# The first stage of a hybrid encoder layer on one core: VectorE's order, the order of the loads, and twenty identity products

## The chip, the cores and the metric

The kernel runs on one core of a Trainium2 chip. The metric is the device time of one execution in microseconds (us). The median of three runs before the change is 2615.54 us, from 2612.58 to 2616.66.

## The reference, cut to what matters

One layer: a layer norm whose scale and shift come from a conditioning vector, one wide input projection, two mixing branches, an output projection, and a second norm.

```python
c_act = jax.nn.silu(c)
mod = c_act @ ada_w[l] + ada_b[l]                      # (1, 3072)
shift, scale, gate = jnp.split(mod, 3, axis=-1)
h = (_layernorm(x) * (1.0 + scale[:, None, :]) + shift[:, None, :]).astype(x.dtype)
proj = h @ w_in[l]                                     # (2048, 9216)
...
y_hg = _hgrn2_branch(q_h, i_h, zf_fw, zf_bw, g_h, ...)  # gated linear recurrence, 8 heads
o_na = _neighbourhood_attention(q_n, k_n, v_n, rpb[l])  # 16 heads, done in 8 pairs
y = jnp.concatenate([y_hg, y_na], axis=-1) @ w_out[l]
x = (_layernorm(DEEPNORM_ALPHA * x + gate[:, None, :] * y) * ln_g[l] + ln_b[l])
```

There are 2048 tokens of width 1024. Every projection is done in three passes for precision: an operand is split into a high part `hi` (its rounded copy) and a low part `lo` (the rest), and the products hi·hi, hi·lo and lo·hi are summed.

## The kernel before, in words

The span of 2610.9 us falls into a first stage (`startup`, until about 98 us), the neighbourhood attention of the first token half, the recurrence, the attention of the second half, and the output projection. The change touches `startup` alone.

`startup` makes the normed, modulated input `h` of the first 1024 tokens, and uses it as it comes. The tokens are in two groups of 512, g = 0 and 1, each of four rows of 128 tokens; the width is cut into eight blocks k = 0 to 7 of 128. For a group there are four x tiles for each half a of the width (a = 0 serves k = 0 to 3, a = 1 serves k = 4 to 7).

What is done for one (g, k):

- `turn_`: four PE transposes of the x tiles into PSUM (L232).
- `high`: ScalarE applies the modulation's `scale1[k]` and `shift[k]` (L237), and copies the result to the high part of h (L239).
- `low`: VectorE subtracts, which gives the low part of h (L1223).
- `block(g, k)`: nine products of 128x512 for the k, q and gate columns of the first pair of attention heads, by L278, into accumulators `acc`.
- one piece of `vproj`, the value projection, twelve products of 128x256 (L291).

PE runs in the order of the program. In iteration (g, k) the program first runs `jobs[g, k]`, then `ahead()`, that is `turn_`, `high` and `low` of the *next* (g, k), and then the block and the value piece of this one. So the next h is made on ScalarE and VectorE while PE works on this one. At (0, 7) come also fourteen products for the next pair's weights (`fourth_mm`, L1281), and the second group's rates and scaling.

What the jobs hold:

- `mod_sum(k)`: VectorE's row sums of a 128x2048 tile of modulation weights, in two instructions (L154), which give `shift[k]` and `scale1[k]`. `high(g, k)` waits for it.
- `w_split(i, a)`: ScalarE's copy (L1199) and VectorE's subtraction (L1200) for half a of the weights of column group i (three groups, six splits).
- `feed.split`: the same for a tile of the value weights (L825, L826); it also issues the load of a later tile.
- `stat`, `rates`, `scale`: the norm. `stat(g, i)` is VectorE's statistics of row i (L202, L203), `rates` the small work on mean and variance, `scale` normalizes x tiles in place, on ScalarE (L225) for rows below its third argument and on VectorE (L227) for the others.

Inside this stage PE, SP, ScalarE and VectorE are held to the program's order:

```python
with phase("st", SB_, SMS), tc.manual_schedule(engines={getattr(mybir.EngineType, e) for e in ("PE", "SP", "Activation", "DVE")}):
    raws, feed, first = startup()
with phase("n0", NB0, SM0):
    natten_init(4, 0)
    st = first_half(raws, feed, first)
```

All loads go through SP's queue. In the stages behind it only PE is held to the program; for the other engines a planner orders the instructions by a timeline of its own (`schedule_with_timeline_sim=True`), and it may place such instructions between those of the first stage.

The modulation tiles `ada` have four buffers. The first holds a diagonal used early, `mod_load(0)` to `(2)` take the others, `mod_load(3)` the first again, and `mod_load(4)` to `(7)` each wait for the `mod_sum` four places earlier.

Of the kernel before, what the change touches and what calls it, by code (L numbers as in the profile page):

```python
# [19 lines left out]
P = 128  # L20
# [18 lines left out]
def body(ctx: ExitStack, tc: tile.TileContext, t):  # L39
    nc = tc.nc  # L40
    dve, act, pool, pe = nc.vector, nc.scalar, nc.gpsimd, nc.tensor
# [46 lines left out]
    def nm(s):  # L88
        cnt[0] += 1
        return f"{s}_{cnt[0]}"  # L90

    def tl(tag, dt=F32, shape=None):
        if tag in cur["smap"]:
            tag = cur["smap"][tag]
            return sh.tile([P, 512], dt, tag=tag, name=nm(tag), bufs=SH[tag])
        return cur["pool"].tile([P, 512] if shape is None else shape, dt, tag=tag, name=nm(tag), bufs=cur["bufs"].get(tag, 1))
# [4 lines left out]
    def ps(tag="mx"):  # L101
        if tag == "pj":
            return pp.tile([P, 512], F32, tag=tag, name=nm("pj"))
        tag = cur["map"].get(tag, tag)
        return cur["psum"].tile([P, 512], F32, tag=tag, name=nm("ps"), bufs=cur["ps"][tag])
# [4 lines left out]
    ident = cp.tile([P, P], F32, name="ident")  # L110
# [36 lines left out]
    def mod_load(k):  # L147
        mod["w", k] = tl("ada", shape=[P, 2 * D])
        dma(mod["w", k], t["ada_m"][k])

    def mod_sum(k):
        for s, (dst, bias) in enumerate(((shift, adab), (scale1, adab1))):
            w, c = mod["w", k][:, s * D:(s + 1) * D], slice(k, k + 1)
            dve.tensor_tensor_reduce(w, w, mod["c"], scale=1.0, scalar=bias[:, c], op0=ALU.mult, op1=ALU.add, accum_out=dst[:, c])  # L154
# [34 lines left out]
    def x_load(g, rows=range(4)):  # L189
        xs = []  # L190
        for i in rows:
            xt = [tl("x"), tl("x")]
            r0 = g * GRP + i * P
            for a in range(2):
                dma(xt[a], x[r0:r0 + P, a * 512:(a + 1) * 512])
            xs.append(xt)
        return xs
# [14 lines left out]
    def x_mv():  # L212
        return cp.tile([P, 4, 2], F32, tag="xmv", name=nm("xmv"), bufs=2)
# [972 lines left out]
    def startup():  # L1186

        dma(adab, t["ada_b"])
        ws = [([], []) for _ in NCOL0]
        wraw = [[tl("raw"), tl("raw")] for _ in NCOL0]  # L1190
        feed = Chunks(first_srcs())

        def w_load(a):
            for i in range(3):
                dma(wraw[i][a], t["w_in"][NCOL0[i][1] // P][:, a * 512:(a + 1) * 512])

        def w_split(i, a):
            hi, lo = tl(f"w{i}", F32R), tl("w2l" if i == 2 else f"w{i}", F32R)
            act.activation(hi, wraw[i][a], AF.Copy)  # L1199
            dve.tensor_tensor(lo, wraw[i][a], hi, op=ALU.subtract)  # L1200
            ws[i][0].append(hi)
            ws[i][1].append(lo)

        mod_silu()
        xs, mvs, how, pts, tmps = {0: x_load(0)}, {0: x_mv()}, {}, {}, {}
        mod_load(0)
        w_load(0)
        feed.load(1)
        mod_load(1)
        mod_load(2)  # L1210
        feed.load(2)
        mod_load(3)
        w_load(1)
        feed.load(3)

        def turn_(g, k):
            pts[g, k] = h_turn(xs[g], k)

        def high(g, k):
            tmps[g, k] = h_high(pts[g, k], k, hts[g, k, 0], True)  # L1220

        def low(g, k):
            dve.tensor_tensor(hts[g, k, 1], tmps[g, k], hts[g, k, 0], op=ALU.subtract)  # L1223

        def stat(g, i):
            x_stat(mvs[g], xs[g], i)

        def rates(g):
            how[g] = x_rates(mvs[g])

        def scale(g, a, n, rows=range(4)):
            x_scale(xs[g], how[g], a, n, rows)

        for i in range(4):
            stat(0, i)
        rates(0)
        scale(0, 0, 4)
        mod_sum(0)

        jobs = {  # L1240
            (0, 0): [(w_split, 1, 0), (w_split, 2, 0), (feed.split, 0), (mod_sum, 1), (mod_sum, 2)],
            (0, 1): [(feed.split, 0), (scale, 0, 1, 4, (0, 1)), (mod_sum, 3)],
            (0, 2): [(w_split, 0, 1), (scale, 0, 1, 4, (2, 3))],
            (0, 3): [(mod_sum, 4), (w_split, 1, 1), (w_split, 2, 1)],
            (0, 4): [(feed.split, 0), (mod_sum, 5)],
            (0, 5): [(mod_sum, 6), (stat, 1, 0), (feed.split, 0)],
            (0, 6): [(lambda: fourth_split(),), (mod_sum, 7), (stat, 1, 1)],
            (0, 7): [(stat, 1, 2), (stat, 1, 3), (rates, 1), (scale, 1, 0, 2)],
            (1, 2): [(scale, 1, 1, 4)],
        }  # L1250
        mod_load(4)
        xs[1], mvs[1] = x_load(1, (0, 1)), x_mv()
        feed.load(4)
        mod_load(5)
        xs[1] += x_load(1, (2, 3))
        mod_load(6)
        mod_load(7)
        acc = {(0, 0): ps("sc"), (1, 0): ps("sc"), (2, 0): ps("po")}
        values = vproj(t["w_v"][0], nv_d[0], 0, feed, True)
        rows = {n: [None, None] for n, _ in NCOL0}  # L1260
        order = [(g, k) for g in range(2) for k in range(KT)]
        fourth, fraw = ([], []), [tl("raw"), tl("raw")]
        for a in range(2):
            dma(fraw[a], t["w_in"][NCOL0[0][1] // P + 1][:, a * 512:(a + 1) * 512])

        def fourth_split():
            w = tl("ada", F32R, [P, 2 * D])
            for a in range(2):
                hi, lo = (w[:, o:o + 512] for o in (a * 512, D + a * 512))
                act.activation(hi, fraw[a], AF.Copy)  # L1270
                fourth[0].append(hi)
                fourth[1].append(lo)

        def fourth_low():
            for a in range(2):
                dve.tensor_tensor(fourth[1][a], fraw[a], fourth[0][a], op=ALU.subtract)

        def fourth_mm(pz, k, low):
            wh, wl = (w[k // 4][:, (k % 4) * P:(k % 4 + 1) * P] for w in fourth)
            for n, (a, b) in enumerate(((wl, hts[0, k, 0]),) if low else ((wh, hts[0, k, 0]), (wh, hts[0, k, 1]))):  # L1280
                pe.matmul(pz, a, b, start=(k + n + low == 0), stop=(low == 1 and k == KT - 1))  # L1281

        def block(g, k):
            for i in (2, 0, 1) if g else (0, 1, 2):
                proj_mm(acc[i, g], *ws[i], g, k)
                if k == KT - 1:
                    rows[NCOL0[i][0]][g] = evac(acc[i, g])

        turn_(0, 0)
        high(0, 0)  # L1290
        w_split(0, 0)
        low(0, 0)
        for n, (g, k) in enumerate(order):
            if (g, k) == (0, 7):
                pz = ps("po")
                for kx in range(KT - 1):
                    fourth_mm(pz, kx, 0)
                block(g, k)
            for f, *a in jobs.get((g, k), []):
                f(*a)  # L1300
            nxt = order[n + 1] if n + 1 < len(order) else None

            def ahead():
                if nxt:
                    turn_(*nxt)
                    high(*nxt)
                    low(*nxt)

            if (g, k) != (0, 7):
                ahead()  # L1310
            if (g, k) == (0, 7):
                feed.load(8)
                rp = bias_rows()
                bias_fill()
                dma(lg, t["lb_logits"])
                dma(normg, t["hg_norm_g"])
            if (g, k) == (1, 0):
                acc.update({(2, 1): ps("po"), (0, 1): ps("sc"), (1, 1): ps("sc")})
                bias_tables(rp)
                bias_pair(0)  # L1320
                dma(c_d.rearrange("(p k) -> p k", k=KT), mod["c8"])
            if (g, k) != (0, 7):
                block(g, k)
            if (g, k) == (0, 7):
                next(values)
                fourth_mm(pz, k, 0)
                fourth_low()
                ahead()
                for kx in range(KT):
                    fourth_mm(pz, kx, 1)  # L1330
                first = evac(pz)
                next(values)
            else:
                next(values, None)
            if g:
                feed.tick()
        for _ in values:
            pass
        return rows, feed, first
# [98 lines left out]
    with psum_phase("n0", NPS), tc.manual_schedule(engines={mybir.EngineType.PE}):  # L1438
        with phase("st", SB_, SMS), tc.manual_schedule(engines={getattr(mybir.EngineType, e) for e in ("PE", "SP", "Activation", "DVE")}):
            raws, feed, first = startup()  # L1440
# [151 lines left out]
    with psum_phase("n1", NPS), phase("n1", NB1, SM1), tc.manual_schedule(engines={mybir.EngineType.PE}):  # L1592
# [13 lines left out]
        feed = Feed(cts)  # L1606
# [95 lines left out]
```

## Time and profile before

| | us |
|---|---|
| median of three runs | 2615.54 |
| lowest, highest | 2612.58, 2616.66 |
| the profiled execution's own time | 2612.69 |
| its span, first to last instruction | 2610.9 |
| PE busy, share of the span | 2561.6, 98% |
| PE busy in the first 100 us | 80.62 |
| VectorE busy in the first 100 us | 62.48 |
| ScalarE busy in the first 100 us | 56.74 |
| modulation weights loaded in the first stage | 8 tiles of 1024 KB |

In rows of the timeline the columns are the start in us, the duration in us, the engine (PE TensorE's matmuls, PEld its weight loads, DVE VectorE, ACT ScalarE, SPq SP's queue), the line of the kernel, the operation, what it writes and reads, and, in brackets, how long the engine was idle just before and what ended that. A row with x3 merges three instructions that follow each other. A row of the chain of waits gives start, length and what the chain went through. A row of the stretches gives the length, and for each engine busy us and instructions, then the granted TensorE clock (PEclk), the DMA engines' share, and GB/s.

### The profile page before, as it was taken

What the parts mean: (1) busy time and instruction counts of PE and PEld (TensorE: products, weight loads), DVE (VectorE), ACT (ScalarE), POOL (GpSimd) and SP (SyncE); (2) the same over time, 40 slices, a digit from 0 to 9 for tenths busy, and PEclk for the clock granted to TensorE, in tenths of its full rate; (3) what the DMA queues carried; (4) which work ended last, traced back from release to release, by engine and by line L of the source; (5) the groups of instructions that cost most, each with busy time, mean ns of one, the idle gap of its engine ahead of it and who ended that gap; (6) DMA issues with size and microseconds to landing.
All of it is one profiled execution on the core that took longest, in us unless ns stands there. A gap on an engine that the chain in (4) does not pass through costs nothing.

```text
span 2610.9 us, 45808 instructions
## 1 busy us (share of the span) xinstructions
PE 2561.6 (98%) x17140; PEld 2146.3 (82%) x17140; DVE 1737.8 (67%) x4356; ACT 1435.4 (55%) x2859; POOL 108.4 (4%) x143
## 2 busy tenths in 40 slices
PE   7999999999999999999999999999999999999998
PEld 5788788878888888888888888898888887788887
DVE  7445545377777778877887777555777778558443
ACT  5533444376666666666766666455777777431110
POOL 0000000000000000000000000000000000042221
PEclk9999999999999999999999999999999999999999
DMA  7576454212111126212212222345455556443331
GB/s 282 149 205 150 129 175 152 95 46 74 62 65 61 62 73 219 81 53 78 65 63 68 74 77 74 112 126 153 127 139 135 147 143 171 125 151 129 97 97 56
DMA packets 225919, 296.40 MB, mean 114 GB/s; under 512 B 28839, under 2 KB 117543, under 8 KB 224551
## 3 DMA queue, kind: packets, MB, share of 16 engines
q1 hardware_dynamic: 225695, 293.46, 37.0%
q8 instruction: 135, 2.21, 0.4%
q14 instruction: 89, 0.73, 0.1%
HBM read 218.18 MB, written 66.99 MB: 109 GB/s over the span
## 4 chain that ended last, share of the span: by engine, by line
PE 90%; DVE 4%; DMA 3%; ACT 2%; issue 1%; SPq 0%; DVEq 0%; ACTq 0%
PE pj L278 51%; PE pj L291 5%; PE ps L1527 4%; PE ps L1528 4%; PE ps L1529 4%; PE ps L1112 3%; PE ps L1090 3%; PE ps L482 2%; PE ps L1041 2%; PE ps L474 2%; PE ps L549 1%; PE ps L573 1%; PE ps L1048 1%; PE ps L575 1%; PE ps L521 1%; PE ps L653 1%
## 5 line engine op out<-in xcount | busy, mean ns | idle before, releaser
L278 PE MATMUL pj<-h,wh 128*128 128x512 f32 x3984 | 1269.9, 400 | 3.6 <-ACT wh L825 1.9
L278 PEld LDWEIGHTS pj<-h,wh 128*128 128x128 f32 x3984 | 722.7, 188 | 155.5 <-issue 14.0
L278 PE MATMUL pj<-h,wl 128*128 128x512 f32 x1992 | 781.2, 392 | 0.0
L278 PEld LDWEIGHTS pj<-h,wl 128*128 128x128 f32 x1992 | 374.5, 188 | 83.3 <-DVE wl L826 0.4
L1062 ACT ACTIVATE pbuf<-pbuf,mx 128x480 f32<-128x480 f32 (+5 forms) x256 | 152.4, 597 | 107.6 <-DVE mx L1057 106.6
L291 PE MATMUL pj<-wh,h 128*128 128x256 f32 x1024 | 196.2, 286 | 0.6 <-ACT vt L299 0.3
L1057 DVE CUSTOM_DVE_ANT_1 pbuf<-ps,bias 128x480 f32<-128x480 f32 (+5 forms) x256 | 129.1, 540 | 99.3 <-PE ps L1046 43.8
L291 PEld LDWEIGHTS pj<-wh,h 128*128 128x128 f32 x1024 | 163.3, 192 | 4.4 <-issue 1.3
L269 DVE TENSOR_TENSOR wl<-wr,wh 128x512 fp32r<-128x512 f32 x192 | 131.2, 684 | 48.2 <-ACT wh L268 46.6
L268 ACT ACTIVATE wh<-wr 128x512 fp32r<-128x512 f32 x192 | 120.2, 626 | 74.4 <-PE pj L278 66.8
L291 PE MATMUL pj<-wl,h 128*128 128x256 f32 x512 | 144.9, 283 | 0.0
L1096 ACT ACTIVATE pt<-ps 120x384 f32<-120x384 f32 (+3 forms) x128 | 65.2, 509 | 121.0 <-PE ps L1090 120.7
L1090 PE MATMUL ps<-ident,pbuf 128*128 128x128 f32 (+2 forms) x832 | 113.5, 274 | 4.0 <-DVE pbuf L1067 3.1
L1094 DVE COPY pt<-ps 120x384 f32<-120x384 f32 (+3 forms) x128 | 74.9, 585 | 63.5 <-PE ps L1090 62.3
L1090 PEld LDWEIGHTS ps<-ident,pbuf 128*128 128x128 f32 (+2 forms) x832 | 97.2, 137 | 22.1 <-issue 2.5
L468 DVE TENSOR_TENSOR de<-e,de 128x512 f32<-128x512 f32 x64 | 44.2, 691 | 95.2 <-ACT de L467 95.2
L1503 ACT ACTIVATE yh<-yr 128x512 fp32r<-128x512 f32 x52 | 32.7, 628 | 131.9 <-PE ps L1528 114.7
L1067 DVE TENSOR_SCALAR pbuf<-pbuf,mx 128x480 f32<-128x480 f32 (+5 forms) x256 | 101.0, 412 | 3.8
L1576 DVE TENSOR_TENSOR vt<-ps,gt 128x512 f32<-128x512 f32 x24 | 16.5, 691 | 129.2 <-PE ps L1529 129.2
L774 ACT ACTIVATE e<-pj 128x512 f32<-128x512 f32 x97 | 57.8, 596 | 80.4 <-PE pj L278 73.7
L291 PEld LDWEIGHTS pj<-wl,h 128*128 128x128 f32 x512 | 98.2, 192 | 1.4 <-issue 0.5
L449 DVE TENSOR_TENSOR_SCAN c<-c,g 128x128 f32<-128x128 f32 x256 | 88.4, 404 | 10.7 <-ACT c L439 10.7
(281 smaller groups left out, 4694.1 us busy)
## 6 DMA issues: line engine op xcount, KB each, us to landing
wr<-in_w_in SPq DMA_DIRECT2D x276, 256.0 KB
yr<-yq SPq DMA_DIRECT2D x64, 256.0 KB
bias<-tint SPq DMA_DIRECT2D x24, 480.0 KB
x<-in_x SPq DMA_DIRECT2D x32, 256.0 KB
ada<-in_ada_m SPq DMA_DIRECT2D x8, 1024.0 KB
wr<-in_w_v SPq DMA_DIRECT2D x32, 256.0 KB
nv<-vt SPq DMA_DIRECT2D x32, 256.0 KB
hs<-s SPq DMA_DIRECT2D x32, 256.0 KB
```

Of the source, the lines that this page charges most:

```text
L268: act.activation(hi, raw, AF.Copy)
L269: dve.tensor_tensor(lo, raw, hi, op=ALU.subtract)
L278: pe.matmul(pz, a, b, start=(k == 0 and n == 0), stop=(k == KT - 1 and n == 2))
L291: pe.matmul(pzs[tp][:, i * 256:(i + 1) * 256], a, b, start=(k == 0 and n == 0 and i == 0), stop=(k == KT - 1 and n == 2), skip_group_check ...
L449: dve.tensor_tensor_scan(c[:, sl], c[:, sl], L[:, sl], 0.0, op0=ALU.add, op1=ALU.subtract)
L1057: return dve.tensor_tensor_reduce(s[:, 0:nk].rearrange("p (r c) -> p r c", c=kw), sc[:, 0:nk].rearrange("p (r c) -> p r c", c=kw), bt[:, 0 ...
L1062: act.activation(s[:, 0:nk], s[:, 0:nk], AF.Exp, scale=-1.0, bias=mx[:, 0:1], accum_out=mx[:, 1:2])
L1067: dve.tensor_scalar(s[:, 0:nk], s[:, 0:nk], mx[:, 2:3], 1.0, op0=ALU.mult, op1=ALU.mult)
L1090: pe.transpose(ptp[0:cw, c * P:(c + 1) * P], s[:, c * cw:(c + 1) * cw], ident)
L1527: pe.matmul(pz, yh[:, kk], wh, start=first, stop=False)
L1528: pe.matmul(pz, yh[:, kk], wl, start=False, stop=False)
L1529: pe.matmul(pz, yl[:, kk], wh, start=False, stop=last)
```

## The change

Four things, all in `startup`:

1. The first four x tiles (a = 0, group 0) are scaled by ScalarE (rows 0 and 1) and VectorE (rows 2 and 3), not all by ScalarE. The second group's a = 1 tiles are scaled by VectorE, two at (1, 1) and two at (1, 2), not four by ScalarE at (1, 2).
2. The jobs stand in another order. The splits of the first two weight groups and `mod_sum(1)` come ahead of the first `low`; `mod_sum(2)` to `(7)`, the other splits and the statistics move between iterations.
3. `mod_load(6)` and `(7)` are issued ahead of the second group's rows 2 and 3.
4. In iteration (0, 0), behind the transposes of k = 1 and ahead of block (0, 0), PE computes 20 products of the 128x128 identity with itself, in float32, into a part of `acc[0, 0]`, which the block's first product then overwrites.

```diff
-        scale(0, 0, 4)
+        scale(0, 0, 2)
         mod_sum(0)
 
         jobs = {
-            (0, 0): [(w_split, 1, 0), (w_split, 2, 0), (feed.split, 0), (mod_sum, 1), (mod_sum, 2)],
-            (0, 1): [(feed.split, 0), (scale, 0, 1, 4, (0, 1)), (mod_sum, 3)],
-            (0, 2): [(w_split, 0, 1), (scale, 0, 1, 4, (2, 3))],
-            (0, 3): [(mod_sum, 4), (w_split, 1, 1), (w_split, 2, 1)],
-            (0, 4): [(feed.split, 0), (mod_sum, 5)],
-            (0, 5): [(mod_sum, 6), (stat, 1, 0), (feed.split, 0)],
-            (0, 6): [(lambda: fourth_split(),), (mod_sum, 7), (stat, 1, 1)],
+            (0, 0): [(w_split, 2, 0), (feed.split, 0)],
+            (0, 1): [(mod_sum, 2), (feed.split, 0), (scale, 0, 1, 4), (mod_sum, 3)],
+            (0, 2): [(mod_sum, 4)],
+            (0, 3): [(w_split, 0, 1), (w_split, 1, 1), (w_split, 2, 1), (feed.split, 0)],
+            (0, 4): [(mod_sum, 5), (mod_sum, 6)],
+            (0, 5): [(mod_sum, 7)],
+            (0, 6): [(feed.split, 0), (lambda: fourth_split(),), (stat, 1, 0), (stat, 1, 1)],
             (0, 7): [(stat, 1, 2), (stat, 1, 3), (rates, 1), (scale, 1, 0, 2)],
-            (1, 2): [(scale, 1, 1, 4)],
+            (1, 1): [(scale, 1, 1, 0, (0, 1))],
+            (1, 2): [(scale, 1, 1, 0, (2, 3))],
         }
         mod_load(4)
         xs[1], mvs[1] = x_load(1, (0, 1)), x_mv()
         feed.load(4)
         mod_load(5)
-        xs[1] += x_load(1, (2, 3))
         mod_load(6)
         mod_load(7)
+        xs[1] += x_load(1, (2, 3))
...
+        w_split(0, 0)
+        w_split(1, 0)
         turn_(0, 0)
         high(0, 0)
-        w_split(0, 0)
+        mod_sum(1)
         low(0, 0)
...
             if (g, k) != (0, 7):
                 ahead()
+            if (g, k) == (0, 0):
+                for _ in range(20):
+                    pe.matmul(acc[0, 0][:, 0:P], ident, ident, start=True, stop=True, skip_group_check=True)
```

## The prediction

> **What bounds the kernel now.** I read the page first (busy shares), then the stretches of the first 60 us, then the timeline of PE, VectorE and ScalarE there, then the chain of waits.
>
> ```profile
> span 2610.9 us, 45808 instructions
> PE 2561.6 (98%) x17140; PEld 2146.3 (82%) x17140; DVE 1737.8 (67%) x4356; ACT 1435.4 (55%) x2859; POOL 108.4 (4%) x143
> 0.00:20.00 20.00, 6.95 (x13) 2.93 (x13) 11.19 (x27) 8.87 (x17) 1.33 (x10) 1.00 0.84 316
> 20.00:40.00 20.00, 18.51 (x101) 15.98 (x101) 18.31 (x31) 12.02 (x20) 0.00 (x0) 1.00 1.04 405
> ```
>
> PE is busy for 98% of the span, so the whole kernel is PE-bound, and only PE's idle or slow time can be won. 13.05 of the 49.3 us without PE work lie in the first 20 us. From 20 to 40 us VectorE is nearly full (18.31 of 20) and the DMA engines are full (1.04). Three limits stand close together there.
>
> ```profile
> 17.02 1.33 PE L232 MATMUL ps<-ident,x 128*128 128x128 f32 x5 [0.23 <-ACT x L225]
> 20.87 1.22 PE L278 MATMUL ps<-h,bk 128*128 128x512 f32 x2 [0.54 <-DVE h L1223]
> 24.45 0.41 PE L291 MATMUL pj<-wh,h 128*128 128x256 f32 x1
> 25.73 0.28 PE L291 MATMUL pj<-wl,h 128*128 128x256 f32 x1
> 28.11 0.73 PE L278 MATMUL ps<-h,bk 128*128 128x512 f32 x2 [0.95 <-DVE h L1223]
> 39.73 0.94 PE L278 MATMUL ps<-h,bk 128*128 128x512 f32 x3
> 43.68 1.35 PE L278 MATMUL ps<-h,bk 128*128 128x512 f32 x3
> 49.30 0.73 PE L278 MATMUL ps<-h,bk 128*128 128x512 f32 x2 [0.58 <-DVE h L1223]
> 55.88 0.84 PE L278 MATMUL ps<-h,bk 128*128 128x512 f32 x3
> ```
>
> These are starts of blocks. Block (0, 0) runs from 20.87, and a value product takes 0.41 us at 24.45 but 0.28 us at 25.73: TensorE worked at a slower rate until about 25.5 us, 4.6 us after its dense work began. Block (0, 1) could go on only at 28.11, when VectorE delivered its low part. Block (0, 5) at 43.68 needs 1.35 us for three products where (0, 4) needs 0.94, a wait of 0.41 us. At 49.30 block (0, 6) waits for VectorE too. In between PE never waits.
>
> ```profile
> 71.78 0.60 PE L232 MATMUL ps<-ident,x 128*128 128x128 f32 x4
> 74.29 0.28 PE L291 MATMUL pj<-wh,h 128*128 128x256 f32 x1
> 75.72 0.60 PE L232 MATMUL ps<-ident,x 128*128 128x128 f32 x4
> 79.52 0.28 PE L291 MATMUL pj<-wh,h 128*128 128x256 f32 x1
> 72.52 2.92 ACT L225 ACTIVATE x<-x,xb,xr 128x512 f32<-128x512 f32 x4
> ```
>
> An undisturbed iteration takes 75.72 - 71.78 = 3.94 us; from its transposes to the value piece are 74.29 - 71.78 = 2.51 us. The next one needs 79.52 - 75.72 = 3.80 us: 1.29 us are lost, since `high(1, 3)` stood behind four scalings on ScalarE (72.52 for 2.92 us).
>
> **The change, part by part.** *The start.* The rows of ScalarE and VectorE:
>
> ```profile
> 14.04 2.93 ACT L225 ACTIVATE x<-x,xb,xr 128x512 f32<-128x512 f32 x4 [1.02 <-DVE xb L209]
> 17.54 0.78 ACT L237 ACTIVATE sg<-ps,shift,scale 128x512 f32<-128x512 f32 x1 [0.57 <-PE ps L232]
> 18.34 0.63 ACT L239 ACTIVATE h<-sg 128x512 fp32r<-128x512 f32 x1
> 25.13 0.78 ACT L237 ACTIVATE sg<-ps,shift,scale 128x512 f32<-128x512 f32 x1 [4.08 <-DVE scale L154]
> 20.13 0.68 DVE L1223 TENSOR_TENSOR h<-sg,h 128x512 fp32r<-128x512 f32 x1
> 20.74 0.68 DVE L1200 TENSOR_TENSOR q<-e,q 128x512 fp32r<-128x512 f32 x1
> 26.16 1.28 DVE L154 CUSTOM_DVE_ANT_0 ada<-ada,nb,adab 128x1024 f32<-128x1024 f32 x1
> 27.37 0.68 DVE L1223 TENSOR_TENSOR h<-sg,h 128x512 fp32r<-128x512 f32 x1
> 59.96 1.00 DVE L227 TENSOR_SCALAR x<-x,xmv,xr 128x512 f32<-128x512 f32 x2
> ```
>
> From them: a scaling is 0.73 us on ScalarE and 0.50 on VectorE; a subtraction occupies VectorE for 0.61 us (20.13 to 20.74), half a `mod_sum` for 1.21 (26.16 to 27.37), a whole one 2.42; `high` takes 0.80 + 0.63 = 1.43.
>
> After the change VectorE scales two tiles from 14.0 to 15.0 and then does `mod_sum(0)` until 17.45. ScalarE scales the other two until 15.5, then copies two weight tiles until about 16.7 (0.6 us each, like L239's copy). So the transposes end earlier, but `high(0, 0)` now waits for `mod_sum(0)` and starts at 17.5, as before (17.54): nothing won by that edit itself. VectorE goes on: two weight subtractions until 18.7, `mod_sum(1)` until 21.1, `low(0, 0)` until 21.8, one us later than before (20.13 + 0.68 = 20.81). But `scale1[1]` is there at 21.1, not just before 25.13, so `high(0, 1)` ends at 22.6, VectorE's two subtractions come between, and `low(0, 1)` ends at 23.6, not at 28.05 (27.37 + 0.68). Block (0, 1)'s wait of 0.95 us goes.
>
> *The loads.* `mod_sum(1)` needs its tile by 18.7.
>
> ```profile
> x<-in_x SPq DMA_DIRECT2D x32, 256.0 KB
> ada<-in_ada_m SPq DMA_DIRECT2D x8, 1024.0 KB
> 26.68 7.79 DMA ada<-in_ada_m
> ```
>
> In the queue's order there stand eight x tiles, `ada` 0, four tiles of 256 KB, `ada` 1 and `ada` 2: 6.3 MB, and 20 us at 316 GB/s is 6.3 MB. So `ada` 2 lands near 20 us and `ada` 1, 1.05 MB earlier, near 17.4: in time, by 1.3 us. The chain has the load issued at 26.68, `ada` 5, landing at 34.47. With 6 and 7 now right behind it, at 405 GB/s (2.6 us each), they land near 37.1 and 39.7; their sums start near 40.2 and 43.3. The second group's rows 2 and 3, pushed back 5.2 us to about 42.3, are read only behind 49 us. SP's queue now holds `mod_load(7)` behind `mod_sum(3)` (near 29.1), and x rows, the fourth group's tiles and later value tiles stand behind it; a load issued at 26.68 lands only 7.79 us later, so the engines have work until SP goes on, and it costs nothing.
>
> *The identity products.* The trace has float32 products of 128x128x128 in the recurrence, two records each:
>
> ```profile
> 870.11 1.06 PE L482 MATMUL ps<-v,ke 128*128 128x128 f32 x8
> 871.00 0.60 PE L474 MATMUL ps<-ident,de 128*128 128x128 f32 x4
> ```
>
> Four products in 871.00 - 870.11 = 0.89 us: 0.223 us each at the full rate, 0.445 at half. Twenty cost 4.46 or 8.9 us. The transposes take (1.33 - 0.45) / 4 = 0.22 us at that hour, so eight from 15.0, two of them held by ScalarE, end near 17.15, and the products follow at once. If the rate rises 4.6 us after dense work begins, as at 25.5 before, 10.3 products run slowly, 9.7 fast, and the last ends at 17.15 + 4.6 + 2.16 = 23.9. They end 2.1 us *behind* the low part that block (0, 0) needs (21.8): this is a cost, paid for by the block's full rate. Block (0, 0), value piece and transposes then take 3.94 us, and block (0, 1) starts at 27.84. Before, it ran as if begun at 28.11 - 0.23 = 27.88 (0.23 us a product, (0.94 - 0.47) / 2). So far nothing won or lost. Bounds: all twenty fast, block (0, 0) at 21.8, 2.1 us better; all slow (26.05) and a slow block behind (20.87 to 26.33, 5.46, and 0.35), 4.0 us worse; all slow with a fast block, 2.15 worse. I take 23.9, from the one ramp that the trace shows.
>
> [...]
>
> *Blocks (0, 2) to (0, 7).* Before, from 27.88 to 55.88 are 28.00 us, of which 0.41 were lost at (0, 5) and 1.04 at (0, 6) (its second product was due at 43.68 + 0.41 + 3.94 + 0.23 = 48.26 and came at 49.30). Without waits block (0, 7) starts 26.55 us behind block (0, 1). VectorE's order allows it: low parts end near 30.0, 33.8, 37.8 for blocks due at 31.8, 35.7, 39.7. Then `mod_sum` 5 and 6 hold VectorE from 37.8 to 42.7, `low(0, 5)` ends at 43.3, and its product is due at 43.8: half a us of cover, the thinnest place. (0, 6): 46.4 against 47.8. Block (0, 7) starts at 27.84 + 26.55 = 54.39, not 55.88: 1.49 won. Behind it the second group's rates still wait for ScalarE's evacuations of that block, so this chain moves along unchanged.
>
> *Second group.* Without four scalings in front, `high(1, 3)` is in time; VectorE takes them, two by two for 1.00 us, where it stands idle. 1.29 won. What is late next is block (1, 7), below.
>
> **The sum:** -1.49 - 1.29 = -2.8 us. The profiled execution took 2612.69 (1.8 us around the span), so 2609.9; against the median of runs, which lies 2.85 above that execution, 2615.54 - 2.8 = **2612.7**. With the bounds, -4.9 to +1.2: 2610.6 to 2616.7.
>
> **The rivals.**
>
> ```profile
> 93.34 0.63 ACT L239 ACTIVATE h<-sg 128x512 fp32r<-128x512 f32 x1
> 94.02 0.50 PE L278 MATMUL ps<-h,vt 128*128 128x512 f32 x1 [1.11 <-ACT h L239]
> 547.22 1.16 PE L482 MATMUL ps<-v,ke 128*128 128x128 f32 x8 [0.80 <-ACT ke L476]
> 554.00 1.61 PE L482 MATMUL ps<-v,ke 128*128 128x128 f32 x8 [2.18 <-ACT ke L476]
> 556.64 1.51 PE L521 MATMUL ps<-qx,kx 128*32 128x64 f32 x64 [1.03 <-DVE kx L512]
> PE pj L278 <- ACT wh L825: 1.9, 1, 1.9
> 274.60:278.10 3.50, 3.50 (x10) 2.40 (x9) 0.96 (x4) 0.27 (x1) 0.00 (x0) 0.51 0.75 243
> 554.50:561.40 6.90, 5.87 (x78) 4.84 (x78) 6.90 (x19) 5.06 (x12) 0.00 (x0) 0.51 0.04 12
> ```
>
> *The planner's order improves (faster).* Behind the first stage ScalarE's and VectorE's order is planned from a simulated timeline that this change shifts. That order leaves waits: one of 1.9 us behind which the granted clock was halved for 3.5 us (together 3.6), and 0.80 + 2.18 + 1.03 = 4.0 us near 550 with 6.9 us of halved clock (together 7.4). If one goes: 2612.7 - 3.6 = 2609.1 to 2612.7 - 7.4 = 2605.3. Against: most of that order hangs on data, which move together.
>
> *The planner's order gets worse (slower).* The same mechanism the other way: a planned instruction set in front of one for which PE waits, as at 93.34, where the copy for block (1, 7) came 1.11 us late. One new place of the larger size gives 2612.7 + 7.4 = 2620.1, two give 2627.5. Slower than before from 2.8 us lost, by over 0.2% (5.2 us) from 8.0. For it: at 98% PE busy the present order leaves little to win and much to lose. Against: as above.
>
> *The identity products eat it.* They end at 26.05, the block behind them fast or slow: -2.8 + 2.15 = -0.65 to +1.2, 2614.9 to 2616.7. The rows can't exclude it: 0.445 is doubled, not seen.
>
> **How the numbers follow.** Forecast 0.48 (0.40 within 0.2%, which is about what a measurement of this kernel can tell from no change; 0.08 faster, at its better bound with a good draw of runs); planner better 0.28, faster; planner worse 0.18 (0.14 slower, 0.04 within); products eat it 0.06, within. Faster 0.36, same 0.50, slower 0.14. The forecast's own range is 2609 to 2618, its bounds with 1.5 us for the runs' spread. The range given reaches to 2605.5 and 2620: it leaves out two new waits and the largest gain, some 0.2.
>
> **What would show it.** Right: `high(0, 0)` near 17.5, identity products from 17 to about 24, block (0, 1) near 27.8 with no wait for VectorE, block (0, 7) 1.5 us earlier than 55.88, no wait of PE for L239 in block (1, 3). Wrong: products that end behind 25, `mod_sum` waiting for a load, block (0, 5) waiting for `low`, or stretches behind 100 us in which PE's idle time or granted clock differ from before by more than the first 100 us do.

## The result and the profile after

| | before | after |
|---|---|---|
| median, us | 2615.34 (2610.53 to 2616.9, 12 runs) | 2609.15 (2604.77 to 2611.98, 12 runs) |
| the profiled execution's own time, us | 2612.69 | 2611.2 |
| its span, us | 2610.9 | 2609.4 |

The ratio of after to before is 0.9977, 95% interval 0.9969 to 0.9986: 3.7 to 8.1 us faster. The forecast was 2612.7, 2.8 us faster, which lies outside that interval. So the sign and the place are right, and the size is too small. The page of after:

```profile
span 2609.4 us, 45888 instructions
PE 2565.7 (98%) x17180; PEld 2153.9 (83%) x17180; DVE 1741.0 (67%) x4362; ACT 1432.1 (55%) x2853; POOL 108.3 (4%) x143
```

It shows almost nothing: 40 records more on PE (twenty products), and PE still at 98%. The stretches say more:

```profile
0.00:20.00 20.00, 8.91 (x27) 6.04 (x28) 14.38 (x33) 8.52 (x16) 1.33 (x10) 1.00 0.86 317
20.00:40.00 20.00, 20.00 (x132) 18.28 (x131) 18.52 (x31) 11.16 (x18) 0.00 (x0) 1.00 1.02 406
```

From 20 to 40 us PE is busy for all of 20.00 us (before: 18.51), and VectorE has done 3 us more of its work by 20 us (14.38 against 11.19). PE's timeline of after, the starts of blocks:

```profile
14.70 0.45 PE L232 MATMUL ps<-ident,x 128*128 128x128 f32 x1 [5.61 <-ACT x L225]
16.86 6.51 PE L1316 MATMUL ps<-ident 128*128 128x128 f32 x40
23.13 0.94 PE L278 MATMUL ps<-h,bk 128*128 128x512 f32 x3
27.07 0.95 PE L278 MATMUL ps<-h,bk 128*128 128x512 f32 x3
42.86 0.95 PE L278 MATMUL ps<-h,bk 128*128 128x512 f32 x3
46.80 0.94 PE L278 MATMUL ps<-h,bk 128*128 128x512 f32 x3
53.59 0.84 PE L278 MATMUL ps<-h,bk 128*128 128x512 f32 x3
73.44 0.60 PE L232 MATMUL ps<-ident,x 128*128 128x128 f32 x4
77.38 0.60 PE L232 MATMUL ps<-ident,x 128*128 128x128 f32 x4
95.46 0.73 PE L278 MATMUL pj<-h,wh 128*128 128x512 f32 x2 [0.62 <-ACT vt L299]
```

The identity products fill PE from 16.86 to 23.13, and block (0, 0) follows at the full rate (0.94 us for three products, where before two took 1.22). From there on no block of the first group waits in this trace: they come 3.94 us apart, (0, 5) and (0, 6) included, and (0, 7) starts at 53.59 (before: 55.88). In the second group the transposes ahead of blocks (1, 3) and (1, 4) are 3.94 us apart too. Before, they stood at 75.72 and 80.94, 5.22 us apart. The last row is the first product behind the stage. The two rows of before:

```profile
80.94 0.60 PE L232 MATMUL ps<-ident,x 128*128 128x128 f32 x4
99.04 0.73 PE L278 MATMUL pj<-h,wh 128*128 128x512 f32 x2 [0.62 <-ACT vt L299]
```

So the stage ends 3.58 us earlier in this pair of traces. VectorE's and ScalarE's rows of after:

```profile
15.74 1.28 DVE L154 CUSTOM_DVE_ANT_0 ada<-ada,nb,adab 128x1024 f32<-128x1024 f32 x1
18.70 1.28 DVE L154 CUSTOM_DVE_ANT_0 ada<-ada,nb,adab 128x1024 f32<-128x1024 f32 x1 [0.46 <-DMA ada<-in_ada_m]
21.11 0.69 DVE L1223 TENSOR_TENSOR h<-sg,h 128x512 fp32r<-128x512 f32 x1
42.15 0.69 DVE L1223 TENSOR_TENSOR h<-sg,h 128x512 fp32r<-128x512 f32 x1
17.13 0.78 ACT L237 ACTIVATE sg<-ps,shift,scale 128x512 f32<-128x512 f32 x1 [0.83 <-PE ps L232]
```

The first row is the second half of `mod_sum(0)`, which ends at 17.02. `mod_sum(1)` waits 0.46 us for its tile. `low(0, 0)` is there at 21.80, `low(0, 5)` at 42.84, 0.25 us ahead of its product (42.86 + 0.23).

Behind the stage every engine issues the same instructions in the same order in both traces; the planner changed nothing there.

### The profile page after: what moved, and what is told of

It is laid out like the page before. It is cut to its first block, busy times and chain, and to the rows that moved or that the text cites. A ratio compares the mean times of both kernels' runs of the same rounds, so it can differ in the third digit from the quotient of the medians.

```text
span 2609.4 us, 45888 instructions
## 1 busy us (share of the span) xinstructions
PE 2565.7 (98%) x17180; PEld 2153.9 (83%) x17180; DVE 1741.0 (67%) x4362; ACT 1432.1 (55%) x2853; POOL 108.3 (4%) x143
## 4 chain that ended last, share of the span: by engine, by line
PE 93%; DVE 3%; DMA 2%; ACT 2%; issue 0%; SPq 0%; DVEq 0%; ACTq 0%
PE pj L278 52%; PE pj L291 6%; PE ps L1534 4%; PE ps L1535 4%; PE ps L1533 4%; PE ps L1112 3%; PE ps L1090 3%; PE ps L482 2%; PE ps L474 2%; PE ps L1041 2%; PE ps L549 1%; PE ps L278 1%; PE ps L573 1%; PE ps L1048 1%; PE ps L521 1%; PE ps L575 1%
```

## The experiments

All times are set against a mark inside the trace, the first transpose (T0, the 14.70 above), since T0 itself moves between 13.96 and 15.00 us from trace to trace with the arrival of the x tiles (VectorE's statistics wait for them until 8.61 us in before, until 7.83 and 9.01 in after). The table has each run's start of block (0, 1) and of block (0, 7), and of the first product behind the stage, behind T0.

| kernel | median, us | before beside it | ratio (95%) | T0 | (0, 1) | (0, 7) | end of stage |
|---|---|---|---|---|---|---|---|
| before | | | | 15.00 | 11.68 | 40.88 | 84.04 |
| before_again | 2614.01 | 2613.47 | 0.9998 (0.9989 to 1.0007) | 14.98 | 11.63 | 40.90 | 84.02 |
| after | 2609.15 | 2615.34 | 0.9977 (0.9969 to 0.9986) | 14.70 | 12.37 | 38.89 | 80.76 |
| after_again | 2607.14 | 2612.51 | 0.9984 (0.9976 to 0.9993) | 14.27 | 11.54 | 38.26 | 80.17 |
| after_third | 2607.35 | 2613.47 | 0.9977 (0.9967 to 0.9988) | 14.69 | 11.65 | 38.79 | 80.65 |
| no_products | 2611.11 | 2612.51 | 0.9994 (0.9985 to 1.0003) | 13.99 | 13.36 | 39.89 | 81.76 |
| scale_on_act | 2609.22 | 2612.51 | 0.9989 (0.9981 to 0.9997) | 14.23 | 11.12 | 37.81 | 80.97 |
| old_loads | 2610.75 | 2612.51 | 0.9996 (0.9987 to 1.0006) | 14.16 | 11.73 | 43.36 | 85.23 |
| before_scale | 2608.91 | 2613.22 | 0.9987 (0.9978 to 0.9996) | 14.18 | 11.62 | 40.90 | 82.78 |
| before_products | 2611.32 | 2613.22 | 0.9991 (0.9982 to 1.0000) | 14.49 | 12.33 | 40.90 | 85.58 |
| products_40 | 2611.63 | 2613.22 | 0.9994 (0.9985 to 1.0003) | 14.33 | 16.60 | 43.10 | 84.98 |
| early | 2612.11 | 2613.22 | 0.9997 (0.9988 to 1.0005) | 14.72 | 10.12 | 40.07 | 86.10 |
| early2 | 2617.04 | 2613.47 | 1.0017 (1.0008 to 1.0026) | 13.96 | 9.88 | 42.25 | 87.43 |
| products_14 | 2609.23 | 2612.30 | 0.9987 (0.9978 to 0.9996) | 14.16 | 11.52 | 38.27 | 80.14 |

In before and the kernels with its order, block (0, 1) begins with one product and then waits for its low part (0.95 us in before), so this column compares only kernels with the new order.

The intervals are 4 to 6 us wide, and what the parts are worth is of that size. So the table's right half, taken from one trace each, tells the parts apart, and the medians only say whether the whole agrees.

### The same kernel again, and the kernel before against itself

The kernel after the change, run again in two other sessions, and the kernel before under a new label (a blank line added to each file; the diff has nothing else).

> The changed kernel once more, for a second trace. Theory A (the gain is made in the first stage alone, and the rest of the 6.2 us is where TensorE's half-rate stretches happen to fall): the first product behind the stage (L278 into pj) starts at 95 to 97 us, against 99.04 before; the half-rate stretches behind 100 us fall elsewhere than in the first trace; the ratio of times is 0.9985, that is 4 us, give or take 2. Theory B (the change also removes half-rate stretches later on): as many as five of them do not come again, the trace has three or fewer, and the ratio stays at 0.9977 or below.

> The changed kernel a third time, beside the control. Theory A: the first product behind the stage starts 80.2 to 80.8 us behind the first transpose, as in the two other traces, and the ratio is 0.9980 to 0.9990. Theory C: the same trace, and a ratio nearer to 0.9975.

> The kernel before once more, as a control and for a second trace of it. Open is why every variant so far, those too whose first stage is longer in the trace, measured 1 to 3 us under the kernel before. Theory A (chance, and the fall of the half-rate stretches): ratio 1.0000 within its interval, block (0, 7) at 40.9 us behind the first transpose as in the first trace. Theory C (the kernel before often ramps up later than its one trace shows, and loses some 2 us by it): the ratio is 1.0000 too, but the trace shows the rate rising later than 25.5 us, or block (0, 7) later than 41.5 us behind the first transpose. Theory D (the order of the measurement favours the second kernel): a ratio near 0.999.

Measured: the kernel before against itself gives 0.9998, so the order in which kernels are run adds at most 0.11%. The three traces of after end the stage at 80.76, 80.17 and 80.65 behind T0, the two of before at 84.04 and 84.02: the stage is 3.3 to 3.9 us shorter. The three ratios give 4.2 to 6.0 us (0.9984 and 0.9977 of some 2613 us); the differences of the medians are 5.4 to 6.2. Half-rate stretches, those of halved granted clock, didn't reliably get fewer: by the record of that clock both traces of before have four behind the stage, after and after_again six each, after_third three. So theory B of after_again, that the change takes such stretches away, isn't borne out.

### Without the identity products, and with products alone

```diff
-            if (g, k) == (0, 0):
-                for _ in range(20):
-                    pe.matmul(acc[0, 0][:, 0:P], ident, ident, start=True, stop=True, skip_group_check=True)
```

That is no_products, after the change without part 4. before_products adds the same three lines to the kernel before.

> The changed kernel without the twenty identity products. Theory A (they cost about what the faster rate returns): block (0, 0) starts at 21.8 us, when its low part is there, at half rate; block (0, 1) starts at 27.4 to 28.5 against 27.07; the first product behind the stage comes 0.3 to 1.5 us later than 95.46; time 0 to 2 us over the changed kernel. Theory B (the products carry the gain): block (0, 1) starts behind 30 us, or half-rate stretches come later in the first 60 us, and the time is 3 us or more over the changed kernel.

> The kernel before with the twenty identity products alone. Theory A (VectorE's order is what holds block (0, 1)): the products end at 23 to 25 us, block (0, 1) still waits for VectorE until 28.1, and the first product behind the stage moves by 0.5 us at most. Rival B (the products carry the gain): it starts 1.5 us or more earlier, and the time falls by as much or more.

PE's timeline of no_products:

```profile
17.91 0.80 PE L278 MATMUL ps<-h,bk 128*128 128x512 f32 x1 [1.55 <-ACT h L239]
21.36 1.22 PE L278 MATMUL ps<-h,bk 128*128 128x512 f32 x2 [2.65 <-DVE h L1223]
27.35 0.95 PE L278 MATMUL ps<-h,bk 128*128 128x512 f32 x3
```

PE stands idle for 1.55 and 2.65 us, then works block (0, 0) at the slow rate (1.22 us for two products), and block (0, 1) comes 13.36 us behind T0: 1.0 to 1.8 us later than with products. Block (0, 7) is 1.0 to 1.6 later. So in the new order the products are worth 1.0 to 1.6 us, against this one trace without them. And of before_products:

```profile
17.64 5.49 PE L1313 MATMUL ps<-ident 128*128 128x128 f32 x40
22.88 0.94 PE L278 MATMUL ps<-h,bk 128*128 128x512 f32 x3
27.60 0.74 PE L278 MATMUL ps<-h,bk 128*128 128x512 f32 x2 [0.29 <-DVE h L1223]
```

Block (0, 0) runs at the full rate here too, but block (0, 1) waits for VectorE's low part as ever, and block (0, 7) starts at 40.90, like before to 0.02 us. (The end of the stage, 85.58, holds a half-rate stretch near 94.5 us which no other trace of before has.) Products alone shorten nothing up to block (0, 7); VectorE's order is what lets them.

### Forty products and fourteen

```diff
-                for _ in range(20):
+                for _ in range(40):
```

and, in products_14, `range(14)`.

> The changed kernel with forty identity products in place of twenty. Theory A (each product beyond the ramp is paid in full): block (0, 0) starts 20 x 0.223 = 4.5 us later; of this VectorE's and the loads' waits give nothing back, since there are none, so the first product behind the stage comes 4.0 to 4.5 us later than in the traces of the changed kernel, near 99, and the time is 4.5 us over it. Rival: the later blocks have slack towards the loads, and 2 us or less remain.

> 14 identity products in place of 20, all else as after the change. After the change block (0, 0) starts at 23.13, right behind the products, while its low part is there at 21.11 + 0.69 = 21.8. Theory A (the products are six too many): the last six run at the full rate, 6 x 0.223 = 1.3 us, so block (0, 0) starts near 21.9 and runs at the full rate, and block (0, 7) stands 37.3 to 38.0 us behind the first transpose (38.3 to 38.9 in the three traces after the change). From block (0, 5) on less than 1.3 may be left, since mod_sum(6) can't start before its tile lands near 39.5. The median is then 0.6 to 1.3 us below that of after the change: a ratio to before of 0.998 or less. Theory B (the cover at block (0, 5) is used up): PE waits there for the low part for 1 us or more and a half-rate stretch follows, as with the old order of the loads; block (0, 7) then stands 39 us or more behind the first transpose, and the ratio is 0.999 or more. Theory C (the rate rises with the grid of stretches, later than the last product): block (0, 0) runs partly at half rate, block (0, 1) comes as after the change, and nothing is won.

PE's timeline of products_40:

```profile
16.49 10.74 PE L1316 MATMUL ps<-ident 128*128 128x128 f32 x80
26.99 0.94 PE L278 MATMUL ps<-h,bk 128*128 128x512 f32 x3
```

Block (0, 1) comes 16.60 us behind T0, 4.2 to 5.1 later than with twenty: twenty more at 0.223 us are 4.46. So products beyond the moment at which the low part is there cost their full price here. Fewer should then win. PE's timeline of products_14:

```profile
16.32 4.06 PE L1316 MATMUL ps<-ident 128*128 128x128 f32 x28
21.93 0.74 PE L278 MATMUL ps<-h,bk 128*128 128x512 f32 x2 [1.31 <-DVE h L1223]
41.46 1.17 PE L278 MATMUL ps<-h,bk 128*128 128x512 f32 x3
45.64 0.95 PE L278 MATMUL ps<-h,bk 128*128 128x512 f32 x3
```

Now block (0, 0) waits for VectorE (1.31 us), and block (0, 5) too (1.17 us where 0.94 is the norm, and 4.18 to the next block instead of 3.94). Blocks (0, 1) and (0, 7) stand at 11.52 and 38.27, as in after_again (11.54 and 38.26). The gain expected, 0.6 to 1.3 us, isn't there, and the ratio of 0.9987 isn't below that of after. Twenty products are not too many by anything that these runs can tell.

### The second group's scalings

after with ScalarE doing them (scale_on_act), and before with VectorE doing them (before_scale, the reverse edit):

```diff
-            (1, 1): [(scale, 1, 1, 0, (0, 1))],
-            (1, 2): [(scale, 1, 1, 0, (2, 3))],
+            (1, 2): [(scale, 1, 1, 4)],
```

> The changed kernel with the second group's a = 1 tiles scaled by ScalarE again, four at (1, 2). Theory A: block (1, 3) waits for the high part again, 1.29 us lost there, and the first product behind the stage comes 1.2 to 1.4 us later than with the change. Rival: ScalarE has found room by the earlier work, and nothing is lost.

> The kernel before with one part of the change alone: the second group's a = 1 tiles scaled by VectorE, two at (1, 1) and two at (1, 2). Theory A: the first product behind the stage starts 1.29 us earlier than 99.04, near 97.75, and the time falls by 1.3 us (ratio 0.9995). Rival: the wait only moves to block (1, 4) and less than 0.5 us is won.

PE's transposes in scale_on_act:

```profile
71.87 0.60 PE L232 MATMUL ps<-ident,x 128*128 128x128 f32 x4
77.07 0.60 PE L232 MATMUL ps<-ident,x 128*128 128x128 f32 x4
```

5.20 us between them instead of 3.94: the wait of 1.26 us is back. From block (0, 7) to the end of the stage it takes 80.97 - 37.81 = 43.16 us, against 41.86 to 41.91 in the three traces of after: 1.25 to 1.30. In before_scale it is the other way: 82.78 - 40.90 = 41.88, against 43.16 and 43.12 in the two traces of before. This part is worth some 1.24 to 1.30 us in both surroundings. The ratio of before_scale is lower by more, 0.9987 (3.4 us), but its interval reaches down to 1.0 us.

### The order of the loads

```diff
+        xs[1] += x_load(1, (2, 3))
         mod_load(6)
         mod_load(7)
-        xs[1] += x_load(1, (2, 3))
```

> The changed kernel with the second group's rows 2 and 3 loaded ahead of modulation tiles 6 and 7 again. Theory A (tile 6 then lands near 39.8 us, its sum started at 39.74 in the trace; tile 7 near 42.3, its sum at 42.76): VectorE waits under 0.3 us at mod_sum(6), the low part of block (0, 5) is late by that much, and the first product behind the stage moves by 0 to 0.3 us. Rival: the wait at mod_sum(6) is 1 us or more, block (0, 5) loses as much.

VectorE's and PE's rows in old_loads, and SP's row that issues the loads of tiles 6 and 7:

```profile
31.21 1.28 DVE L154 CUSTOM_DVE_ANT_0 ada<-ada,nb,adab 128x1024 f32<-128x1024 f32 x1 [1.58 <-DMA ada<-in_ada_m]
42.29 1.28 DVE L154 CUSTOM_DVE_ANT_0 ada<-ada,nb,adab 128x1024 f32<-128x1024 f32 x1 [2.55 <-DMA ada<-in_ada_m]
45.45 0.73 PE L278 MATMUL ps<-h,bk 128*128 128x512 f32 x2 [2.91 <-DVE h L1223]
33.16 1.00 SPq L149 DMA_DIRECT2D ada<-in_ada_m  x2
```

and the stretch from 45 to 50 us:

```profile
45.00:50.00 5.00, 4.55 (x17) 3.92 (x18) 5.00 (x9) 2.86 (x5) 2.07 (x1) 0.66 0.08 29
```

`mod_sum(4)` waits 1.58 us for its tile and `mod_sum(6)` 2.55. The first need not come of this edit: after_third, with the new order of loads, waits 1.70 us at the same place. Behind the second stands `low(0, 5)`, and for that PE waits 2.91 us. Then PE's granted clock falls: 0.66 on average from 45 to 50 us. Block (0, 7) comes 4.5 to 5.1 us later than after the change, and the stage is longer than before the change (85.23 against 84.04). I had expected 0 to 0.3 us, since I took the tile to land in the order of the bytes in the queue, 2.6 us behind the 37.1 of the prediction for the 1 MB of rows now ahead of it, so near 39.7; its sum could begin only at 42.29. The sum by bytes left out when SP issues the load: here it did so from 33.16 on, behind the x rows, where after issues tiles 5 to 7 in one go from 26.44 to 29.93. How much of the delay that makes, no run tells. By this trace the new order of VectorE can't do without the new order of the loads; the ratio, 0.9996 (0.9987 to 1.0006), can't tell old_loads from before.

### Warming PE earlier

Two tries for a better version. early puts 16 products ahead of the first transposes and 12 at the old place, `low(0, 0)` and the third weight split ahead of `mod_sum(1)`, and one `mod_sum` into each iteration:

```diff
+        warm(16)
         turn_(0, 0)
         high(0, 0)
-        mod_sum(1)
         low(0, 0)
+        w_split(2, 0)
+        mod_sum(1)
...
-            (0, 1): [(mod_sum, 2), (feed.split, 0), (scale, 0, 1, 4), (mod_sum, 3)],
-            (0, 2): [(mod_sum, 4)],
+            (0, 1): [(mod_sum, 2), (feed.split, 0)],
+            (0, 2): [(scale, 0, 1, 4, (0, 1)), (mod_sum, 3)],
...
-                for _ in range(20):
...
+                warm(12)
```

early2 also puts `feed.split` ahead of `mod_sum(1)`, spreads the scalings over (0, 1) and (0, 2), and has GpSimd do the subtractions of the three second-half weight tiles.

> The changed kernel with sixteen identity products ahead of the first transposes, where PE is idle, and twelve at the old place; the low part of (0, 0) ahead of mod_sum(1); and the sums of the modulation tiles spread one to an iteration, the second group's statistics moved to (0, 7). Theory A: block (0, 0) starts at 18.6 to 19.5 at full rate, block (0, 1) near 24.7, then the loads of modulation tiles 5 and 6 are the bound: block (0, 6) starts at 43.5 to 45.5 against 46.8 and 45.7, and the first product behind the stage at 92.5 to 94.5, against 95.46 and 94.44 in the two traces of the changed kernel. Rival: the half rate comes back between the transposes and block (0, 0), and nothing is won.

> The early version mended where its trace showed new waits: the first value tile is split ahead of mod_sum(1), two scalings each at (0, 1) and (0, 2) ahead of the transposes that need them, and the subtractions of the second half of the three weight groups go to GpSimd (1.3 us each, where it is idle). Expected from the rows so far: block (0, 1) 10 to 10.5 us behind the first transpose (11.5 to 12.4 with the change), block (0, 5) bound by the load of modulation tile 5, block (0, 7) at 36.5 to 38 (38.3 to 38.9 with the change), and the first product behind the stage at 78.5 to 80 (80.2 to 80.8). Rival: the statistics, now behind block (0, 6), hold the second group's rates, and the stage is no shorter.

The waits of PE from 14 to 62 us, in early (what waited for what, us in total, times, the longest in us):

```profile
PE ps L232 <- ACT x L225: 5.0, 5, 2.8
PE pj L291 <- DVE wl L826: 2.0, 2, 1.4
```

Block (0, 1) comes 1.4 to 2.3 us sooner, and all of it is given back: PE waits for the split of a value tile (1.4 us) and for scalings, the second group's statistics now stand behind `low(0, 7)`, and its transposes wait 2.8 us (0.95 before). Behind that wait the clock is halved for 3.4 us, as the stretch shows:

```profile
62.90:66.30 3.40, 3.40 (x11) 2.52 (x10) 0.69 (x1) 1.44 (x3) 0.00 (x0) 0.50 0.00 0
```

VectorE's rows in early2, two iterations:

```profile
44.20 0.69 DVE L1223 TENSOR_TENSOR h<-sg,h 128x512 fp32r<-128x512 f32 x1 [1.57 <-ACT h L239]
44.80 1.28 DVE L154 CUSTOM_DVE_ANT_0 ada<-ada,nb,adab 128x1024 f32<-128x1024 f32 x1
48.87 0.69 DVE L1223 TENSOR_TENSOR h<-sg,h 128x512 fp32r<-128x512 f32 x1 [1.57 <-ACT h L239]
```

One `mod_sum` per iteration, directly ahead of the `high` that needs it, makes a chain: 0.60 for the subtraction, 2.5 for the sums, 1.57 of waiting for ScalarE's two operations. That is 4.67 us an iteration (48.87 - 44.20), and PE needs 3.94. The kernel is slower than before, 1.0017. The statistics hold its second group as well: the transposes there wait 2.71 us. Neither beats the change.

## Why the prediction was right, and where it was off

**Right: the two terms, by their mechanism.** The wait in block (1, 3) was put at 1.29 us; taking it out and putting it back measured 1.24 to 1.30, in the surroundings of both kernels. From block (0, 1) to (0, 7) the prediction gave 26.55 us; the trace of after has 53.59 - 27.07 = 26.52, after_again 26.72 and after_third 27.14 (the thinnest place, below). Behind that nothing new was late: the second group's first rates and block (1, 7) moved along.

**Right in time, not in the wait: `high(0, 0)`** was put near 17.5, behind `mod_sum(0)`, and began at 17.13. The trace has it released by PE's transposes; `mod_sum(0)` ended at 17.02, so the two came almost together. **Right: both planner rivals fall.** Behind the stage the order of instructions is the same on all engines, so the planner neither won nor lost anything there. The third rival, that the products eat the gain, falls with no_products: without them the stage is longer.

**Off: the identity products, at nothing.** Twenty products are worth 1.0 to 1.6 us in the new order (no_products). The step that failed is the length of the slow part. I counted the 4.6 us of the one ramp in the trace of before from the first product, 17.15 + 4.6. In four traces with twenty products it ended 1.1 to 3.6 us behind the first product, and 3.3 to 5.8 us behind T0. In before, PE stood idle for 1.20 and 0.54 us between the transposes and the block, and the rate rose 10.5 us behind T0 (25.5 - 15.0); with the products PE doesn't stand idle there. Whether the slow part counts from the transposes, no run shows by itself. The 1.1 to 3.6 us are an estimate: with 20 products lasting D in all, of 0.445 us each while slow (doubled, by the granted clock of 0.50 below) and 0.223 while fast, (D - 4.46) / 0.222 of them ran slowly. PE's rows of scale_on_act:

```profile
14.84 1.76 PE L232 MATMUL ps<-ident,x 128*128 128x128 f32 x7 [0.17 <-ACT x L225]
16.39 5.26 PE L1315 MATMUL ps<-ident 128*128 128x128 f32 x40
21.41 0.94 PE L278 MATMUL ps<-h,bk 128*128 128x512 f32 x3
```

D is 21.41 - 16.39 = 5.02 us, so 2.5 products were slow, and the rate rose some 1.1 us behind the first product. In after D is 6.27: 8.2 slow ones, 3.6 us. In after_again it is 5.44 (4.4, 2.0 us), in after_third 5.54 (4.9, 2.2 us). Counted from T0 that is 3.3, 5.8, 4.1 and 4.3 us. The granted clock can check the last one, in two stretches of after_third:

```profile
14.00:19.00 5.00, 4.14 (x19) 3.88 (x20) 4.53 (x9) 4.15 (x8) 0.00 (x0) 0.50 1.04 421
19.00:20.00 1.00, 1.00 (x9) 1.00 (x9) 1.00 (x3) 0.59 (x2) 0.00 (x0) 0.86 0.94 389
```

The clock is 0.50 until 19 us and 0.86 on average in the next one, so it rises 0.28 us into it, at 19.28: 4.6 us behind T0, 0.3 later than by the products. Where in these 3.3 to 5.8 us the rise falls differs between traces of the same kernel, so how much one execution gains here differs too. Block (0, 1) follows: 11.12, 12.37, 11.54 and 11.65 us behind T0. My value was 27.84 - 15.0 = 12.84, later than any of these. So on average 1.2 us were missing from the sum at this place, of which the thin cover below takes some back.

**The thinnest place, as named, and bounded by a load.** Block (0, 5) was given half a us of cover. After had 0.25; where block (0, 1) starts earlier it is gone. In products_14 block (0, 5) waits 0.23 us, as shown. In after_again `mod_sum(5)` waits 0.20 us for its tile, and block (0, 5) needs 1.13 us for three products. In after_third `mod_sum(4)` waits longer:

```profile
31.34 1.28 DVE L154 CUSTOM_DVE_ANT_0 ada<-ada,nb,adab 128x1024 f32<-128x1024 f32 x1 [1.70 <-DMA ada<-in_ada_m]
```

That trace takes 27.14 us from block (0, 1) to (0, 7), where after takes 26.52. So two of the prediction's signs of being wrong, a `mod_sum` that waits for a load and block (0, 5) waiting for `low`, did appear, at a cost of 0.2 to 0.6 us, and an earlier start is paid back here in part. Block (0, 7) varies by 0.6 us in the three traces of after, block (0, 1) by 0.8.

**Off: the landing of the loads.** `mod_sum(1)`'s tile was to be in time by 1.3 us; VectorE waited 0.46 us for it, with no harm, since the products covered that. The prediction gave the new load order no term of its own. old_loads shows, in one trace, that it carries 4.5 to 5.1 us of the stage: without it the stage is longer than before the change.

**The whole.** By the traces the stage is 3.3 to 3.9 us shorter, against 2.8 predicted: 1.29 right, and the first term, 1.49, 0.5 to 1.1 too small (block (0, 7) comes 1.99, 2.62 and 2.09 us earlier than in before). What each edit of the first group is worth by itself, the split of the first four scalings for one, was not run. The three ratios say 4.2 to 6.0. Their intervals are 3.7 to 8.1, 1.8 to 6.3 and 3.1 to 8.6 us: the stage's gain lies inside the second, and at the lower edge of the other two. Whether there are 1 to 2 us more, and where, stays open. Three kernels whose stage is 0.9 to 2.1 us longer in the trace than before's (old_loads, products_40, early) came out 0.8 to 1.6 us faster than before by the ratio, none of it clear of the noise; the ratios don't follow the stage to 2 us. Behind the stage nothing of it is seen: from its end to the end of the span the traces of before take 2511.9 and 2514.7 us, those of after 2513.9, 2515.5 and 2509.8. That spread of 6 us, under the same order of instructions, is larger than what is sought. Part of it can be seen in the stretches of after:

```profile
2188.30:2191.70 3.40, 3.40 (x12) 2.88 (x11) 3.24 (x9) 2.35 (x7) 0.00 (x0) 0.50 0.84 209
2212.20:2215.60 3.40, 3.14 (x9) 2.63 (x10) 3.11 (x9) 3.14 (x7) 0.00 (x0) 0.50 1.05 196
```

Twice PE's clock was halved there for 3.4 us. The trace of before runs at the full rate at that place:

```profile
2191.70:2195.10 3.40, 3.40 (x28) 2.70 (x30) 3.30 (x11) 2.38 (x7) 0.00 (x0) 1.00 1.07 249
```

These stretches come and go from execution to execution (six behind the stage in after, three in after_third). The wait of 1.9 us for L825 that the prediction names stands near 270 us in all five traces of before and after, but a halved stretch follows it in before, before_again and after (granted clock 0.86 on average from 268 to 280 us), not in after_again and after_third (1.00). So the change doesn't decide it, and this pair of spans differs by 1.5 us only, where the stage differs by 3.58. Over all fourteen traces they go with the time behind the stage: by the record of the granted clock it is halved there for 11 to 16 us in before_scale, old_loads, no_products and after_third, which take 2507.9 to 2509.8 us, and for 28 to 29 us in after and after_again, which take 2513.9 and 2515.5. They don't explain all of it: before and before_again have 22 us each and differ by 2.8. That they also make the medians' extra microseconds is a guess; two of the three traces of after have more halved time than those of before, one has less.

## What to carry to other kernels

A serial start has several limits that lie close together, so parts that win nothing alone (the products in the old order) or lose by themselves (the new order of VectorE on the old order of loads, by its one trace) can win together: cost each edit with the others in place, not one by one against the kernel before. Products that only keep TensorE busy fill time in which it stands idle (1.55 and 2.65 us in no_products); twenty more, behind the point at which the data of the first real product were there, cost their full price (4.2 to 5.1 us). A sum that a block needs is best done an iteration ahead; put directly ahead of its use, as in early2, its whole chain is added up in every iteration (4.67 us, where PE needs 3.94).

## What the runs showed of the hardware

- **TensorE was slow at the start of its dense work, for a time that varied from trace to trace.** In four traces with twenty products the rise came 3.3 to 5.8 us behind the first transpose, worked out from the products, and as early as 1.1 us behind the first product (scale_on_act). The record of the granted clock has it 4.6 us behind the first transpose in after_third, with 0.50 until 19 us, and 6.1 us in after: 0.3 us later than by the products in both. In before the rise came 10.5 us behind the first transpose, and 4.6 us behind the start of block (0, 0). What sets the time, no run shows.
- **The bytes ahead of a load didn't say when it landed.** In old_loads a tile expected near 39.7 us, from the bytes ahead of it, held up VectorE until 42.29. And one load, of modulation tile 4, was issued at 18.74 us in after and at 18.73 in old_loads, with the same loads ahead of it; in after VectorE began its sum at 29.67 without a wait, in old_loads it had to wait until 31.21.
- **VectorE took longer beside GpSimd's subtractions.** Rows of VectorE and GpSimd in early2:

```profile
33.16 1.36 DVE L1223 TENSOR_TENSOR h<-sg,h 128x512 fp32r<-128x512 f32 x1 [1.57 <-ACT h L239]
34.44 2.30 DVE L154 CUSTOM_DVE_ANT_0 ada<-ada,nb,adab 128x1024 f32<-128x1024 f32 x1
32.70 1.27 POOL L1200 TENSOR_TENSOR q<-e,q 128x512 fp32r<-128x512 f32 x1
33.93 1.73 POOL L1200 TENSOR_TENSOR gt<-e,vt 128x512 fp32r<-128x512 f32 x1
```

Beside GpSimd's two subtractions, VectorE's subtraction and half `mod_sum` take 1.36 and 2.30 us; the rows of early2 shown above have 0.69 and 1.28.
